# A two-layer diffusion backbone on one core: the first layer's context attention is interleaved with the first latent block, and some SBUF start addresses move by 128 bytes

## The chip, the cores and the metric

The kernel runs on one core of a Trainium2 chip, as one launch. The metric is device time in microseconds (us). The time before is the median of three runs, 3418.91 us (3416.81 to 3418.94).

The engines are TensorE (PE; its weight loads are listed as PEld), VectorE (DVE), ScalarE (ACT), GpSimd (POOL) and SyncE (SP, which here only issues DMAs). Each engine executes its own instructions in the order of the program.

## What is computed

The trunk has two layers over 1024 latent tokens, with 256 context tokens as a prefix; the model width is 1024, everything is float32. The change lies in layer 0. Its mixer projects the normalised tokens with one large weight, gives part of the columns to grouped-query attention (8 query heads of 64, 2 key heads) and part to a bidirectional gated scan (HGRN2), and multiplies both results with one output projection:

```python
def attend(q, k, v):
    s = jnp.einsum("bqhgd,bkhd->bhgqk", q, k).astype(jnp.float32) * ATTN_SCALE
    p = jax.nn.softmax(s, axis=-1).astype(v.dtype)
    return jnp.einsum("bhgqk,bkhd->bqhgd", p, v)
...
# latent queries: keys of context and latent; context queries: keys of the context alone
y_lat = jnp.concatenate([oa_lat, readout(ob_lat, bg_l)], axis=-1) @ w_out
y_ctx = jnp.concatenate([oa_ctx, readout(ob_ctx, bg_c)], axis=-1) @ w_out
```

So a context query sees 256 keys, and a latent query sees 1280.

## The kernel before

**Stages.** `even_in` normalises the tokens, projects them token by token (`even_token_major`) and then runs the HGRN2 scan (`hgrn`), which projects as it goes. `even_out` holds the attention and the output projection (`even_attention`). `middle` is the first ConvFFN and the entry of layer 1, `odd_out` its output projection, `last` the second ConvFFN. A float32 product is made of three fp32r matmuls (high by high, high by low, low by high), all recorded at the helper line L115.

**The attention (`even_attention`).** Queries come in five blocks of 256: block 0 is the context, blocks 1 to 4 the latents. A pair (b, h) is a block with a head; there are 40 pairs. Each pair takes two half-steps s, one for each 128 queries, and the loop over s from 0 to 87 is a software pipeline written out by hand (`in_order` keeps the order on every engine). In half-step s, in this order on each engine:

- `scores(s)` (L115, DVE L897): the score matmuls of half-step s into PSUM, then one DVE instruction that copies them into the tile `a_p` and gives the row's minimum `nm` (the queries were stored negated). A context half-step writes 256 columns into `g_ps`, of which there are two buffers; a latent one writes 1280 columns into `a_s`, of which there is one, so the next latent scores wait for this DVE instruction;
- `exponential(s-1)` (ACT L904);
- `prepare_w` (ACT L868, POOL L869) in some half-steps: one of eight pieces of the output weight is split into `w_hi` and `w_lo`;
- `values` (tile `a_pv`) for the pair three before;
- `transposes` (PE L930, ACT L931, DVE L932) for the pair two before: a latent half-step transposes ten 128 by 128 pieces in three groups through two PSUM buffers, a context pair four pieces in its first half-step and none in its second. Both halves of the pair must have been divided. Between the groups, `step` may pull work of the output projection;
- `divide(s-1)` (DVE L909, POOL L910): the reciprocal `rl` of the row sum, and one POOL instruction that multiplies all of `a_p` by it;
- `finish` (ACT L959, DVE L961) for the pair three before, in its second half-step, and entries of a list `todo`: `split` (ACT L950, POOL L951) for every second head, and four `gated` for the HGRN2 result once a block's last head is finished.

Six buffers of `a_p` let half-steps overlap.

**The projection as filler.** `project()` is a generator that yields after each three matmuls of the output projection; a block has 32 such yields. `step(n)` advances it, but never beyond the blocks whose `gated` entries have all run (`ready`). If a block's entries come due while the one before is still unfinished, `gated` first pulls the rest at once. The last block's 32 yields come after the loop.

**Order of the pairs before.** All eight context pairs come first (half-steps 0 to 15), then the latent blocks one after the other. The eight `prepare_w` lie in half-steps 2, 4, ... 16. The context block's last head (pair 7) is finished in half-step 21, its fourth `gated` runs in half-step 23, and the projection begins in half-step 24, with two yields in each half-step.

**Addresses.** In `mod_init` a tile `c_in` of 128 bytes per partition lies in the pool that comes ahead of `xh` and `xl`. In `even_attention` a tile `zeros` of 128 bytes (`LINE` is 32 floats) lies ahead of the keys, queries, probabilities and the other tiles of that stage.

Of the kernel before, what the change touches and what calls it, by code (L numbers as in the profile page):

```python
# [11 lines left out]
F32 = mybir.dt.float32  # L12
# [3 lines left out]
OP = mybir.AluOpType  # L16
# [4 lines left out]
P = 128  # L21
D = 1024
KT = D // P
# [7 lines left out]
AQ = 8  # L31
# [8 lines left out]
LINE = 32  # L40
# [21 lines left out]
class Trunk:  # L62
# [100 lines left out]
    def mod_init(self):  # L163
        nc, a = self.nc, self.a
        self.csil = self.mc.tile([P, KT, 32], F32, name="csil")
        c = self.mc.tile([P, KT, 4], F32, name="c_in")[:, :, 0:2]
        nc.sync.dma_start(c, a["cc"])
        nc.vector.memset(self.csil, 0.0)
        nc.scalar.activation(self.csil[:, :, 0:2], c, AF.Silu)
        self.bmt = self.mc.tile([P, DEPTH, 48], F32, name="bmt")  # L170
        nc.sync.dma_start(self.bmt, a["bmodT"])
        self.nrm = self.mc.tile([P, DEPTH, 2, KT], F32, name="nrm")
        nc.sync.dma_start(self.nrm, a["npreT"])
# [658 lines left out]
    def even_attention(self, gp, tp, pp, sp):  # L832
# [5 lines left out]
        nc, a = self.nc, self.a  # L838
        QB = 2 * P
        blocks = [(SEQ, 1)] + [(QB * i, 0) for i in range(4)]  # L840
        pairs = [(b, h) for b in range(len(blocks)) for h in range(AQ)]
        st = {}

        def load_q(i):
            if i < len(pairs):
                b, h = pairs[i]
                q2 = sp.tile([P, QB], F32R, name="a_q", bufs=3)
                nc.sync.dma_start(q2.bitcast(F32), self.q2d[h][:, blocks[b][0]:blocks[b][0] + QB].bitcast(F32))
                st["q", i] = q2

        def load_gate(kind):
            g = st["gate"] = sp.tile([P, D], F32, name="gate", bufs=1)
            nc.sync.dma_start(g, self.gated[0, 0, kind].partition_broadcast(P))
# [5 lines left out]
        def load_w(m):  # L859
            if m < 8:  # L860
                raws[m] = self.wp.tile([P, 1024], F32, name="w_raw", bufs=2)
                k = 2 * (m % 4)
                nc.sync.dma_start(raws[m].rearrange("p (a b) -> p a b", a=2), w_out[:, k:k + 2, 512 * (m // 4):512 * (m // 4) + 512])

        def prepare_w(m):
            raw = raws.pop(m)
            hi, lo = (self.wp.tile([P, 1024], F32R, name="w_" + x, bufs=8) for x in ("hi", "lo"))
            nc.scalar.copy(hi, raw)  # L868
            nc.gpsimd.tensor_tensor(out=lo, in0=raw, in1=hi.bitcast(F32), op=OP.subtract)  # L869
            W[m] = hi, lo  # L870
            load_w(m + 2)
# [3 lines left out]
        def load_keys(g):  # L875
            for s in range(2):
                k = K2[g, s] = sp.tile([P, NTOK], F32R, name=f"K2_{g}{s}", bufs=1)
                nc.sync.dma_start(k.bitcast(F32), self.k2d[g, s].bitcast(F32))
# [22 lines left out]
        def exponential(i):  # L901
            Pt, nm, nk = st["t", i]
            l = st["l", i] = self.small.tile([P, 1], F32, name="l")
            nc.scalar.activation(Pt[:, :nk], Pt[:, :nk], AF.Exp, bias=nm, scale=-1.0, accum_out=l)  # L904
# [43 lines left out]
        def split(b, k, oT):  # L948
            oh, ol = st["o", b, k] = [sp.tile([P, QB], F32R, name=f"a_o{x}", bufs=12) for x in "hl"]
            nc.scalar.copy(oh, oT)  # L950
            nc.gpsimd.tensor_tensor(out=ol, in0=oT, in1=oh.bitcast(F32), op=OP.subtract)  # L951

        def finish(pair):
            b, h = pairs[pair]
            pv = st["pv"]
            if h % 2 == 0:
                st["oT"] = sp.tile([P, QB], F32, name="a_oT", bufs=2)
            t = sp.tile([P, QB], F32, name="pv_t", bufs=1)[64:128]
            nc.scalar.copy(t, pv[64:128, :QB])  # L959
            r = 64 * (h % 2)  # L960
            nc.vector.tensor_tensor(out=st["oT"][r:r + 64], in0=pv[0:64, :QB], in1=t, op=OP.add)  # L961
            if h % 2 == 1:
                todo.append(lambda oT=st["oT"]: split(b, h // 2, oT))
            if h == AQ - 3:
                g = st["g", b] = self.wp.tile([P, BH, QB], F32, name="a_g", tag="w_raw", bufs=2)
                for k in range(BH):
                    nc.sync.dma_start(g[:, k, :], self.hgd[k][:, blocks[b][0]:blocks[b][0] + QB])
            if h == AQ - 1:
                todo.extend(lambda k=k: gated(b, k) for k in range(BH))

        def gated(b, k):

            step(32 * b - at[0])
            split(b, BH + k, st["g", b][:, k, :])
            if k == BH - 1:
                st["ready"] = b
# [37 lines left out]
        fill, todo, at = project(), [], [0]  # L1014

        def step(n):

            for _ in range(n):
                if at[0] < 32 * (st.get("ready", -1) + 1):
                    next(fill, None)  # L1020
                    at[0] += 1

        zeros = sp.tile([P, LINE], F32, name="zeros", bufs=1)[:, 0:1]
        nc.gpsimd.memset(zeros, 0.0)
        N = 2 * len(pairs)
        E = mybir.EngineType
        with self.in_order(*self.compute, E.SP):
            load_keys(0)
            load_q(0)
            load_q(1)  # L1030
            load_keys(1)
            V = sp.tile([P, NT, AKV * P], F32R, name="V2", bufs=1)
            nc.sync.dma_start(V.bitcast(F32), self.v2d.rearrange("t p c -> p t c").bitcast(F32))
            load_w(0)
            load_w(1)
            load_gate(1)
            for s in range(N + 8):
                pair, half = s // 2, s % 2
                if s < N:
                    if half == 0:  # L1040
                        load_q(pair + 2)
                    scores(s)
                if 0 <= s - 1 < N:
                    exponential(s - 1)
                if 2 <= s < 18 and half == 0:
                    prepare_w(s // 2 - 1)
                if 0 <= pair - 3 < len(pairs):
                    values(pair - 3, half)
                t = transposes(pair - 2, half) if 0 <= pair - 2 < len(pairs) else iter(())
                next(t, None)  # L1050
                step(1)
                next(t, None)
                step(1)
                next(t, None)
                if 0 <= s - 1 < N:
                    divide(s - 1)
                if 0 <= pair - 3 < len(pairs) and half == 1:
                    finish(pair - 3)
                for _ in range(min(len(todo), 1 + len(todo) // 3)):
                    todo.pop(0)()  # L1060
            while todo:
                todo.pop(0)()
            step(32)
            for _ in fill:
                pass
# [1257 lines left out]
```

## Time and profile before

| what | us |
| --- | --- |
| median of three runs | 3418.91 |
| the profiled execution's own time | 3424.98 |
| its span, first to last instruction | 3423.0 |
| span: PE busy | 3125.8 (91%) |
| stretch 692 to 728, context scores | PE 20.51, POOL 32.82 busy of 36.00 |
| stretch 728 to 757, first latent scores | PE 21.79, POOL 24.51 busy of 29.00 |
| stretch 757 to 1060, latent blocks with filler | PE 283.75, POOL 228.79 busy of 303.00 |

All times below are counted from the start of the span. A row of the timeline has the start, the duration, the engine, the line, the operation, the tile written and the tiles read, and in brackets the engine's idle time before it with what ended it. A row of groups ends in busy time, mean duration in ns, and idle time before. PEclk is the TensorE clock that was granted, as a share of full speed.

### The profile page before, as it was taken

The numbers are of one execution on the slowest core, as the hardware profiler recorded it, in microseconds if no ns is written. First come the engines' busy times: TensorE is split into PE (matmuls) and PEld (weight loads), VectorE is DVE, ScalarE is ACT, GpSimd is POOL, SyncE is SP. The second block draws the span as 40 slices with busy tenths as digits, with TensorE's granted clock in tenths as the row PEclk, the third lists the DMA queues.
The fourth block names the chain that finished last, engine by engine and source line by source line (L and its number), as shares of the span: only waits on it lengthen the run. The fifth ranks groups of instructions, "written<-read, shape, count | busy, mean of one in ns | idle before, by whom it ended". The sixth has DMA issues, their size and how long they took to land.

```text
span 3423.0 us, 48746 instructions
## 1 busy us (share of the span) xinstructions
PE 3125.8 (91%) x18364; PEld 2575.7 (75%) x18364; DVE 2057.6 (60%) x3413; ACT 1486.6 (43%) x2619; POOL 1524.0 (45%) x1147
## 2 busy tenths in 40 slices
PE   5999998869998699999999989999997679999997
PEld 3766776658887488888878768898986468888785
DVE  3625666647775754545577763476775565454778
ACT  3223222256664543434344442566664344443443
POOL 1310111187774466666610111677771167777201
PEclk8999999979999699999999989999998789999998
DMA  6533333221112221212285772222215412222756
GB/s 233 161 102 128 128 119 115 101 90 38 50 44 67 96 71 64 73 68 73 74 291 190 254 241 112 70 60 64 66 44 172 154 50 88 79 87 80 269 186 215
DMA packets 204844, 399.25 MB, mean 117 GB/s; under 512 B 24112, under 2 KB 86064, under 8 KB 204608
## 3 DMA queue, kind: packets, MB, share of 16 engines
q1 hardware_dynamic: 195552, 364.15, 32.6%
q0 software_dynamic: 9056, 31.99, 2.4%
q8 instruction: 144, 2.36, 0.3%
q14 instruction: 92, 0.75, 0.1%
HBM read 322.11 MB, written 74.34 MB: 116 GB/s over the span
## 4 chain that ended last, share of the span: by engine, by line
PE 74%; DVE 10%; DMA 4%; ACT 4%; issue 4%; POOL 2%; SPq 1%; POOLq 0%; ACTq 0%; DVEq 0%
PE g_ps L115 21%; PE u_g L115 13%; PE d_ps L115 10%; PE u_v L115 10%; PE u_pc L115 4%; PE c_pv L115 2%; PE a_pv L115 2%; PE c_s L115 2%; PE c_pt L2032 2%; PE a_pt L930 2%; PE mod_ps L115 1%; DVE a_pl L932 1%; PE a_s L115 1%; ACT a_ph L931 1%; DMA m_raw<-in_w_mod 1%
## 5 line engine op out<-in xcount | busy, mean ns | idle before, releaser
L123 POOL TENSOR_TENSOR rs_r<-rs_e,mhalf 128x1 f32<-128x1 f32 (+3 forms) x106 | 81.3, 767 | 1015.1 <-DVE rs_e L122 1014.8
L115 PE MATMUL d_ps<-d_Bh,d_Ah 128*128 128x512 f32 x704 | 277.3, 394 | 10.8 <-ACT d_Bh L1460 10.7
L115 PE MATMUL g_ps<-xh,w_hi 128*128 128x512 f32 (+1 forms) x704 | 277.0, 394 | 5.6 <-ACT w_hi L544 5.6
L115 PE MATMUL d_ps<-d_Bl,d_Ah 128*128 128x512 f32 x704 | 277.8, 395 | 3.9 <-DVE d_Bl L1461 3.4
L115 PE MATMUL d_ps<-d_Bh,d_Al 128*128 128x512 f32 x704 | 276.6, 393 | 2.0 <-DVE d_Al L1461 1.9
L910 POOL TENSOR_SCALAR a_p<-a_p,rl 128x1280 f32<-128x1280 f32 (+1 forms) x80 | 240.0, 3003 | 73.1 <-DVE rl L909 64.8
L2015 POOL TENSOR_SCALAR c_p<-c_p,rl 128x640 f32<-128x640 f32 (+1 forms) x128 | 230.8, 1805 | 86.0 <-DVE rl L2014 60.7
L115 PE MATMUL g_ps<-xh,w_lo 128*128 128x512 f32 (+1 forms) x704 | 257.2, 365 | 1.5 <-DVE w_lo L545 1.2
L115 PE MATMUL g_ps<-xl,w_hi 128*128 128x512 f32 (+1 forms) x704 | 256.9, 365 | 0.0
L1242 DVE TENSOR_TENSOR f_u<-u_v,f_p 128x512 f32<-128x512 f32 x88 | 60.5, 687 | 185.4 <-PE u_v L115 185.4
L932 DVE TENSOR_TENSOR a_pl<-a_pt,a_ph 128x512 fp32r<-128x512 f32 (+1 forms) x200 | 118.6, 602 | 85.7 <-ACT a_ph L931 85.3
L115 PEld LDWEIGHTS g_ps<-xh,w_hi 128*128 128x128 f32 x704 | 134.4, 191 | 44.7 <-issue 27.8
L115 PEld LDWEIGHTS d_ps<-d_Bh,d_Ah 128*128 128x128 f32 x704 | 133.6, 190 | 41.1 <-ACT d_Bh L1460 12.3
L115 PEld LDWEIGHTS d_ps<-d_Bl,d_Ah 128*128 128x128 f32 x704 | 133.5, 190 | 36.4 <-DVE d_Bl L1461 8.0
L1228 POOL TENSOR_TENSOR w_S4l<-w_s,w_S4h 128x512 fp32r<-128x512 f32 x44 | 57.0, 1295 | 230.4 <-ACT w_S4h L1227 230.4
L115 PE MATMUL g_ps<-w_hi,xh 128*128 128x512 f32 (+1 forms) x400 | 156.1, 390 | 2.2 <-DVE xh L1797 1.2
L115 PEld LDWEIGHTS d_ps<-d_Bh,d_Al 128*128 128x128 f32 x704 | 133.6, 190 | 30.8 <-DVE d_Al L1461 3.3
L931 ACT CAST a_ph<-a_pt 128x512 fp32r<-128x512 f32 (+1 forms) x200 | 102.8, 518 | 121.7 <-PE a_pt L930 121.4
L115 PE MATMUL g_ps<-w_lo,xh 128*128 128x512 f32 (+1 forms) x400 | 152.0, 380 | 2.7 <-DVE w_lo L1785 1.9
L115 PEld LDWEIGHTS g_ps<-xh,w_lo 128*128 128x128 f32 x704 | 133.7, 190 | 25.0 <-DVE w_lo L545 1.7
L115 PE MATMUL g_ps<-w_hi,xl 128*128 128x512 f32 (+1 forms) x400 | 152.1, 380 | 0.2 <-DVE xl L280 0.2
L2035 DVE TENSOR_TENSOR c_pl<-c_pt,c_ph 128x256 fp32r<-128x256 f32 (+1 forms) x256 | 113.0, 470 | 50.1 <-ACT c_ph L2034 48.9
(468 smaller groups left out, 9738.4 us busy)
## 6 DMA issues: line engine op xcount, KB each, us to landing
m_raw<-in_w_mod SPq DMA_DIRECT2D x96, 512.0 KB
w_raw<-in_w_up SPq DMA_DIRECT2D x88, 512.0 KB
d_rawA<-actd SPq DMA_DIRECT2D x77, 512.0 KB
d_rawB<-in_w_down SPq DMA_DIRECT2D x74, 512.0 KB
actd<-f_t SPq DMA_DIRECT2D x22, 640.0 KB
d_t<-in_w_down SPq DMA_DIRECT2D x22, 512.0 KB
actd<-f_t SPq DMA_DIRECT2D x22, 512.0 KB
d_s<-actd SPq DMA_DIRECT2D x20, 512.0 KB
```

The costliest lines, as they stand in the source:

```text
L115: return self.nc.tensor.matmul(out, lhsT, rhs, start=start, stop=stop, skip_group_check=True, **k)
L123: nc.gpsimd.tensor_tensor(out=r[:p, :n], in0=e[:p, :n], in1=self.mhalf[:p, :n], op=OP.pow)
L910: nc.gpsimd.tensor_scalar(Pt[:, :nk], Pt[:, :nk], rl, None, op0=OP.mult)
L930: nc.tensor.transpose(pt[:, m, qt * P:(qt + 1) * P], Pt[:, kts[j + m] * P:(kts[j + m] + 1) * P], self.ident)
L931: nc.scalar.copy(ph[:, j:j + n], pt[:, :n])
L932: nc.vector.tensor_tensor(out=pl[:, j:j + n], in0=pt[:, :n], in1=ph[:, j:j + n].bitcast(F32), op=OP.subtract)
L1228: nc.gpsimd.tensor_tensor(out=lo, in0=part(j, name), in1=hi.bitcast(F32), op=OP.subtract)
L1242: nc.vector.tensor_tensor(out=out, in0=x, in1=y, op=OP.add)
L2015: nc.gpsimd.tensor_scalar(Pt[:, :n], Pt[:, :n], rl, None, op0=OP.mult)
L2032: nc.tensor.transpose(pt[:, j, :], Pt[:, (src + j) * P:(src + j + 1) * P], self.ident)
L2035: nc.vector.tensor_tensor(out=vap(pl, o, dims), in0=pt[:, :cnt], in1=vap(ph, o, dims).bitcast(F32), op=OP.subtract)
```

## The change

```diff
-        c = self.mc.tile([P, KT, 4], F32, name="c_in")[:, :, 0:2]
+        c = self.wp.tile([P, 1024], F32, name="c_in", tag="w_raw", bufs=self.w_raw)[:, 0:2 * KT].rearrange("p (k s) -> p k s", s=2)
...
-        pairs = [(b, h) for b in range(len(blocks)) for h in range(AQ)]
+
+        pairs = [p for i in range(4) for p in ((0, 2 * i), (0, 2 * i + 1), (1, i))] + [(1, h) for h in range(4, AQ)]
+        pairs += [(b, h) for b in range(2, len(blocks)) for h in range(AQ)]
...
-                st["oT"] = sp.tile([P, QB], F32, name="a_oT", bufs=2)
+                st["oT", b] = sp.tile([P, QB], F32, name="a_oT", bufs=3)
...
-            nc.vector.tensor_tensor(out=st["oT"][r:r + 64], in0=pv[0:64, :QB], in1=t, op=OP.add)
+            nc.vector.tensor_tensor(out=st["oT", b][r:r + 64], in0=pv[0:64, :QB], in1=t, op=OP.add)
...
-                todo.append(lambda oT=st["oT"]: split(b, h // 2, oT))
+                todo.append(lambda oT=st["oT", b]: split(b, h // 2, oT))
...
-        zeros = sp.tile([P, LINE], F32, name="zeros", bufs=1)[:, 0:1]
+        zeros = sp.tile([P, 2 * LINE], F32, name="zeros", bufs=1)[:, 0:1]
...
-                if 2 <= s < 18 and half == 0:
-                    prepare_w(s // 2 - 1)
+                if 2 <= s < 26 and s % 3 == 2:
+                    prepare_w(s // 3)
...
-                step(1)
+                step(1 if at[0] >= 32 else 2)
```

The order of the first twelve pairs becomes: two context heads, one latent head of block 1, four times over; then block 1's other four heads, then blocks 2 to 4 as before. The eight `prepare_w` move to half-steps 2, 5, 8, ... 23. While the context's 32 yields last, a half-step takes three yields instead of two. A third buffer of `a_oT` lets the two blocks be under way together.

The numbering of half-steps stays, so their content changes: the twelve mixed pairs fill half-steps 0 to 23. The context's last head is pair 10 and is finished in half-step 27; its fourth `gated` runs in half-step 29, and the projection begins in half-step 30. In both programs pair 15 is the last of block 1, its first `gated` comes due in half-step 37, and from half-step 38 on the two programs are the same.

The start addresses of the tiles in SBUF, modulo 256 bytes, as the two programs have them:

| tiles | before | after |
| --- | --- | --- |
| weights `w_raw`, `w_hi`, `w_lo` and nearly all large tiles of the later stages | 128 | 128 |
| `xh`, `xl` of layer 0 | 0 | 128 |
| keys `K2`, `V2`, `a_q`, `a_p`, `a_ph`, `a_pl`, `a_oT`, `a_oh`, `a_ol`, `y`, `y_x` of the attention | 0 | 128 |
| HGRN2: `hA`, `hkt`, `hds`, `hS`, `h_dg`, `h_o` | 0 | 128 |
| HGRN2: `hF`, `hK`, `hQ`, `hT`, `hq`, `hKM`, `hV`, `hgate`, `ones` | 128 | 0 |

## The prediction

> **What bounds the kernel now.** I read the page first, then busy time by stretch, then POOL's groups, then the timeline where the context pairs give way to the latent ones. The page gives the span, PE's busy share and the chain that ended last.
>
> ```profile
> span 3423.0 us, 48746 instructions
> ...
> PE 3125.8 (91%) x18364; PEld 2575.7 (75%) x18364; DVE 2057.6 (60%) x3413; ACT 1486.6 (43%) x2619; POOL 1524.0 (45%) x1147
> ...
> PE 74%; DVE 10%; DMA 4%; ACT 4%; issue 4%; POOL 2%; SPq 1%; POOLq 0%; ACTq 0%; DVEq 0%
> ```
>
> PE bounds the whole, so what counts is where PE waits or runs slowly. The stretches, with the busy time of PE, PEld, DVE, ACT and POOL and then PEclk, show it:
>
> ```profile
> 200.00:245.00 45.00, 45.00 (x202) 35.53 (x201) 4.91 (x9) 6.49 (x12) 0.00 (x0) 1.00 0.21 71
> 300.00:420.00 120.00, 112.97 (x1297) 83.42 (x1295) 77.35 (x161) 35.93 (x66) 17.86 (x23) 1.00 0.38 122
> 692.00:728.00 36.00, 20.51 (x85) 16.79 (x84) 14.54 (x60) 21.40 (x53) 32.82 (x28) 0.63 0.54 179
> 728.00:757.00 29.00, 21.79 (x100) 17.96 (x100) 18.19 (x34) 17.25 (x32) 24.51 (x12) 0.76 0.11 33
> 757.00:1060.00 303.00, 283.75 (x1820) 245.76 (x1819) 224.97 (x410) 194.31 (x370) 228.79 (x100) 1.00 0.13 43
> ```
>
> The projections of layer 0 (first two rows) are PE-bound. The context's scores (692 to 728) are POOL-bound: 32.82 of 36.00, with PE busy 20.51 at a clock of 0.63. From 757 on, with the projection as filler, PE is busy 94% at full clock. The change touches the third and fourth rows by its order, and all five by its addresses.
>
> **The order.** After half-step 38 both programs are the same, so I compare when half-step 38 starts its scores. POOL's groups and the rows of the timeline that I use (in the first fence: shapes, count, busy us, mean ns):
>
> ```profile
> L910 POOL TENSOR_SCALAR a_p<-a_p,rl 128x1280 f32<-128x1280 f32 x64 | 225.4, 3522 | 71.7 <-DVE rl L909 63.4 <-ACT a_oh L950 8.1
> L869 POOL TENSOR_TENSOR w_lo<-w_raw,w_hi 128x1024 fp32r<-128x1024 f32 x8 | 18.9, 2365 | 0.3 <-ACT w_hi L868 0.3
> L951 POOL TENSOR_TENSOR a_ol<-a_oT,a_oh 128x256 fp32r<-128x256 f32 x20 | 14.7, 736 | 8.3 <-ACT a_oh L950 8.3
> L910 POOL TENSOR_SCALAR a_p<-a_p,rl 128x256 f32<-128x256 f32 x16 | 14.7, 929 | 1.4 <-DVE rl L909 1.4
> L868 ACT CAST w_hi<-w_raw 128x1024 fp32r<-128x1024 f32 x8 | 8.2, 1030 | 0.0
> ```
>
> ```profile
> 698.13 0.92 POOL L910 TENSOR_SCALAR a_p<-a_p,rl 128x256 f32<-128x256 f32 x1 [1.40 <-DVE rl L909]
> ...
> 702.12 0.77 PE L115 MATMUL g_ps<-K,a_q 128*128 128x256 f32 x2 [4.02 <-DMA a_q<-q2d]
> ...
> 745.79 2.48 PE L115 MATMUL a_s<-K,a_q 128*128 128x512 f32 x6
> ...
> 748.08 1.67 PE L930 MATMUL a_pt<-ident,a_p 128*128 128x128 f32 x8
> ...
> 750.78 1.40 PE L115 MATMUL a_s<-K,a_q 128*128 128x512 f32 x6
> ...
> 752.44 1.49 DVE L897 CUSTOM_DVE_ANT_0 a_p<-a_s,zeros 128x1280 f32<-128x1280 f32 x1
> ...
> 753.06 1.36 ACT L904 ACTIVATE a_p<-a_p,nm 128x1280 f32<-128x1280 f32 x1
> ...
> 753.75 1.04 PE L930 MATMUL a_pt<-ident,a_p 128*128 128x128 f32 x8
> ...
> 755.90 0.44 PE L930 MATMUL a_pt<-ident,a_p 128*128 128x128 f32 x2 [1.11 <-DVE a_pl L932]
> 756.09 1.40 PE L115 MATMUL a_s<-K,a_q 128*128 128x512 f32 x6
> ...
> 760.77 1.42 PE L115 MATMUL a_s<-K,a_q 128*128 128x512 f32 x6
> ...
> 764.10 0.48 PE L115 MATMUL g_ps<-w_hi,a_oh 128*128 128x512 f32 x1
> ...
> 835.97 1.32 PE L115 MATMUL a_s<-K,a_q 128*128 128x512 f32 x6
> ```
>
> Before: half-step 24 starts its scores at 760.77, its first filler runs at 764.10, and half-step 38 starts at 835.97. Without filler a latent half-step takes (760.77 - 750.78)/2 = 5.0. With two yields it takes little more: from 760.77 to 835.97 are 14 half-steps, less the four yields pulled at once in half-step 37 (next fence, 2.80, so 0.70 each), (75.20 - 2.80)/14 = 5.17.
>
> ```profile
> 833.34 2.80 PE g_ps L115 x12
> ```
>
> That is the flaw that I see in the new order: **a latent half-step without filler costs nearly as much as one with it.** It is held by a ring, not by PE's work: from the transpositions to the next scores are 756.09 - 753.75 = 2.34, with 1.11 of waiting for DVE; then 1.40 of scores and 1.49 of DVE. Before, the filler starts with 8 latent half-steps scored; after, with 14 (half-step 30), so six more run bare, and their yields are made up later.
>
> Step by step, after:
> 1. The first latent scores are half-step 4. Their query tile is the one that lands just before 702.12, so its DVE instruction ends about 702.1 + 1.4 + 1.5 = 705.0, and half-step 5 can start its scores, since `a_s` has one buffer.
> 2. From there: exp 1.36 with its row-sum read (about 0.2), `w_hi` 1.03, `w_lo` 2.37 on POOL ahead of the division, two divisions 2 x 3.52: 12.0, at 717.0. Only then can the pair be transposed (half-step 8). PE has two context pairs between, some 5 us of work, and waits for the rest.
> 3. Half-steps 8 and 9 transpose the latent pair beside context scores: about 2.9 each to the next scores (2.34 and 0.5 of context scores). Half-step 10's latent scores and their DVE instruction add 2.5 behind DVE's queue: 8.3, so half-step 11 starts at 725.3.
> 4. This repeats: half-step 17 at 725.3 + 12.8 + 8.3 = 746.4 (ACT has 0.8 of a context pair's copies ahead of the exp), half-step 23 another 21.1 later and 0.7 for the `a_ol` that then stands between the two divisions: 768.2. POOL's own work in such six half-steps is 4 x 0.93 + 2 x 3.52 + 2 x 2.37 + 0.74 = 16.2, so POOL would idle 5 of 21.
> 5. Pair 11 is transposed at 768.2 + 12.8 = 781.0, half-step 27 starts at 783.3, half-step 30 three bare ones later: 798.3.
> 6. Eight half-steps with three yields. The third adds at most its 0.70, and at least 0.70 less PE's idle share of a half-step, (303.00 - 283.75)/57 = 0.34: 5.5 to 5.9, I take 5.8: 46.4. Then 32 - 24 = 8 yields are pulled at once in half-step 37: 5.6. Half-step 38 starts at 850.3.
>
> So the order costs 850.3 - 836.0 = **14**. The bounds: if POOL never idled, its work from 698.13 up to the division of half-step 27 would be 16 x 0.93 + 12 x 3.52 + 8 x 2.37 + 6 x 0.74 = 80.5, half-step 30 could start at 776, and half-step 38 at 776 + 8 x 5.5 + 5.6 = 826: 10 gained. The other end is PE at half clock in those bursts (below): 21 lost. I take the ring's value, since the rows of the same ring (750.78 to 760.77) show it.
>
> The rest of the order costs nothing that I can find: SP is passed the same DMAs, and the output weight is ready by half-step 23, ahead of its first use in 30. The moved `w_lo` are the 2.37 of step 2: in their old places they were in the POOL-bound stretch too, and are counted once.
>
> **The addresses.** The chain of waits shows long runs of 512-column matmuls; the first of these runs has `xh` at 0 modulo 256, the second, in layer 1's entry, the same form with `xh` at 128 (the weights are at 128 in both):
>
> ```profile
> 233.36 16.82 PE g_ps L115 x72
> ```
>
> ```profile
> 2108.02 36.76 PE g_ps L115 x162
> ```
>
> These are 16.82/72 = 0.2336 and 36.76/162 = 0.2269 per matmul, both at full clock: 6.7 ns apart. Nothing else that I know differs in the two runs' instructions. The change puts `xh`, `xl`, the keys and `a_oh` to 128. Matmuls of 512 columns in layer 0's projections:
>
> ```profile
> L115 PE MATMUL g_ps<-xh,w_hi 128*128 128x512 f32 x256 | 109.4, 427 | 0.0
> ...
> L115 PE MATMUL g_ps<-w_hi,xh 128*128 128x512 f32 x160 | 64.8, 405 | 0.9 <-ACT w_hi L479 0.9
> ```
>
> With their two partners each that is 3 x 416 = 1248, times 6.7 ns = 8.4. The short runs inside HGRN2 get only part, so I take 7. The attention has another 736 (256 in the scores, 480 filler), 4.9 at most, but the ring holds there, and I count none. Bounds: 0, if the addresses aren't the reason, and 13. The HGRN2 tiles that go from 128 to 0 feed small matmuls only; no row tells their price, and I count nothing. The sum: 14 - 7 = **7 slower**.
>
> **Against the median.** The profiled execution took 3424.98, 1.98 more than its span; the median of the three runs is 3418.91, 6.07 lower. The sum is a difference inside one execution, so I add it to the median: 3426. About 0.2% (6.8 us) is what a measurement of this kernel can tell from no change.
>
> **Rivals.**
> - *Half clock in the mixed stretch (slower).* PEclk was 0.63 and 0.76 in the two stretches now mixed. At half clock scores take 2.48 instead of 1.40 and from transpositions to the next scores pass 750.78 - 748.08 = 2.70 instead of 2.34, so each group of six half-steps costs 1.1 + 2 x 0.4 = 2 more, and a few bare half-steps 1 each: 7 in all, 3433. For it: PE would be busy about half of each group, with a gap of some 5 us. Against it: the clock was full in 750 to 760 with such bare half-steps. The Trainium skill (TensorE: Matmul & The Clock Gate, "What's actually happening") says that an idle window of about 3.4 us throttles PE to half clock, and a busy one releases it; by that rule the gap of each group would throttle PE.
> - *POOL stays fed (not slower).* One mechanism: the division of the latent half-steps starts early enough that PE never waits for it, because POOL's queue is filled ahead by the six `a_p` buffers. It decides in step 2: if the transpositions of half-step 8 begin within 8 us of half-step 5's scores rather than 12, each group is 16 to 17 instead of 21, half-step 38 comes at 829 to 832, 4 to 7 early; with the addresses 3406. For it: POOL ran without a gap from 698 to 733 before. Against it: `rl` of each division stands behind the transpositions' DVE work.
> - *The addresses do nothing (slower).* The 6.7 ns come from something else in layer 0, and the order's 14 stand alone: 3433. The Trainium skill (same page, "Wait — 56ns, not 53.3ns?") gives the warm spacing of matmuls as columns over 2.4 GHz plus 2.5 ns, by my estimate 216 ns for 512, and knows no address; the two runs above, 234 and 227, agree neither with that nor with each other.
>
> **How the numbers follow.** My forecast as worked out, 3426: 0.40, its own spread half below and half above 0.2%. Half clock 0.18, slower. Addresses without effect 0.12, slower. POOL fed 0.30, nearly all faster (0.27). So faster 0.27, within 0.2% 0.23, slower 0.50. The range, 3405 to 3437, reaches from the fed POOL to the half clock with weak addresses.
>
> **What would show it.** Right: in the new profile the latent transpositions of half-steps 8, 14, 20 wait for POOL `a_p` L910, the mixed groups take about 21 us each, half-step 30's first filler runs near 800, half-step 38's scores start about 14 later than 835.97 less what was gained ahead, and a run of 72 matmuls near 233 takes 16.3. Wrong: groups of 17 or less, or filler before 790 would mean the ring was misread; a run of 72 still at 16.8 would mean that the addresses are not the cause; PEclk of 0.5 through the groups is the first rival.

## The result and the profile after

The changed kernel is slower: its median of five runs is 3437.70 us against 3418.91, and the ratio is 1.0052 (95% interval 1.0040 to 1.0065, that is 14 to 22 us). One of the five runs was disturbed (6420.15); the other four took 3431.36 to 3438.56, with their middle at 3435.6. The profiled execution took 3431.36, with a span of 3429.5. The page's span and busy times, after:

```profile
span 3429.5 us, 48743 instructions
...
PE 3111.9 (91%) x18364; PEld 2566.0 (75%) x18364; DVE 2060.2 (60%) x3413; ACT 1487.1 (43%) x2619; POOL 1524.7 (44%) x1147
```

PE is busy 13.9 us less than before (3125.8), and yet the span is longer, so PE waits more. The stretches shown of before, after the change (PE, PEld, DVE, ACT, POOL, then PEclk), and two more within the last one:

```profile
200.00:245.00 45.00, 45.00 (x207) 36.31 (x206) 4.08 (x8) 6.38 (x11) 0.00 (x0) 1.00 0.23 77
300.00:420.00 120.00, 113.98 (x1337) 84.09 (x1336) 80.42 (x165) 36.36 (x66) 19.22 (x25) 1.00 0.40 127
692.00:728.00 36.00, 22.42 (x102) 18.77 (x103) 17.18 (x49) 19.53 (x40) 23.77 (x17) 0.67 0.35 115
728.00:757.00 29.00, 15.54 (x92) 12.80 (x90) 13.12 (x37) 16.34 (x36) 23.09 (x13) 0.85 0.25 78
757.00:1060.00 303.00, 275.16 (x1733) 237.68 (x1734) 217.72 (x398) 188.40 (x361) 227.47 (x103) 0.99 0.14 46
```

```profile
765.00:798.00 33.00, 23.56 (x149) 19.77 (x149) 22.74 (x44) 21.85 (x42) 28.07 (x14) 1.00 0.07 21
798.00:850.00 52.00, 50.83 (x306) 43.82 (x305) 33.73 (x62) 30.22 (x58) 37.02 (x18) 1.00 0.17 52
```

The first row shows the addresses: in the same 45 us PE got through 207 recorded matmuls instead of 202. The fourth shows the order: PE is busy 15.54 of 29.00, where it had been 21.79, and POOL isn't full either (23.09). From 765 to 798 PE is still idle for 9.4 of 33 us; from then on, with the filler, it is busy 50.83 of 52.00.

What PE waited for between 692 and 765, by the view of waits (total, times, longest):

```profile
PE a_pt L932 <- POOL a_p L912: 11.2, 5, 3.9
PE a_pv L115 <- DVE a_oT L963: 9.6, 6, 2.5
PE a_s L115 <- DMA a_q<-q2d: 4.0, 1, 4.0
```

The timeline of PE after shows where: a latent pair's transpositions (tile `a_pt`) wait for POOL's division once in each group of six half-steps.

```profile
697.91 2.50 PE L115 MATMUL a_s<-K,a_q 128*128 128x512 f32 x6 [4.01 <-DMA a_q<-q2d]
702.00 2.50 PE L115 MATMUL a_s<-K,a_q 128*128 128x512 f32 x6 [0.74 <-DVE nm L899]
713.87 1.75 PE L932 MATMUL a_pt<-ident,a_p 128*128 128x128 f32 x7 [3.16 <-POOL a_p L912]
...
723.45 1.43 PE L115 MATMUL a_s<-K,a_q 128*128 128x512 f32 x6
...
736.12 1.75 PE L932 MATMUL a_pt<-ident,a_p 128*128 128x128 f32 x7 [3.17 <-POOL a_p L912]
...
745.37 1.41 PE L115 MATMUL a_s<-K,a_q 128*128 128x512 f32 x6
...
758.78 1.76 PE L932 MATMUL a_pt<-ident,a_p 128*128 128x128 f32 x7 [3.86 <-POOL a_p L912]
...
768.27 1.41 PE L115 MATMUL a_s<-K,a_q 128*128 128x512 f32 x6
...
781.01 0.98 PE L932 MATMUL a_pt<-ident,a_p 128*128 128x128 f32 x7 [1.29 <-POOL a_p L912]
783.21 1.41 PE L115 MATMUL a_s<-K,a_q 128*128 128x512 f32 x6
...
797.13 1.41 PE L115 MATMUL a_s<-K,a_q 128*128 128x512 f32 x6
800.47 0.48 PE L115 MATMUL g_ps<-w_hi,a_oh 128*128 128x512 f32 x1
...
849.18 1.30 PE L115 MATMUL a_s<-K,a_q 128*128 128x512 f32 x6
```

The `a_s` rows at 702.00, 723.45, 745.37 and 768.27 are half-steps 5, 11, 17 and 23; those at 783.21, 797.13 and 849.18 are 27, 30 and 38. The groups take 21.9 and 22.9 us. POOL's own rows for the first of them show what PE waits for. `w_lo` stands ahead of the pair's two divisions, which end at 706.79 + 2 x 3.52 = 713.83, and PE goes on at 713.87 (the third of the row's x3 is a context division behind them):

```profile
704.45 2.38 POOL L871 TENSOR_TENSOR w_lo<-w_raw,w_hi 128x1024 fp32r<-128x1024 f32 x1 [0.68 <-ACT w_hi L870]
706.79 7.92 POOL L912 TENSOR_SCALAR a_p<-a_p,rl 128x1280 f32<-128x1280 f32 x3
```

To compare the attention alone I use the first instruction of VectorE's minimum as a mark (the first one, half-step 0, and the one of half-step 38). Timeline of before, then of after:

```profile
696.76 0.42 DVE L897 CUSTOM_DVE_ANT_0 a_p<-g_ps,zeros 128x256 f32<-128x256 f32 x1 [2.37 <-POOL zeros L1024]
...
837.44 1.49 DVE L897 CUSTOM_DVE_ANT_0 a_p<-a_s,zeros 128x1280 f32<-128x1280 f32 x1 [2.72 <-PE a_s L115]
```

```profile
692.44 0.42 DVE L899 CUSTOM_DVE_ANT_0 a_p<-g_ps,zeros 128x256 f32<-128x256 f32 x1 [2.37 <-POOL zeros L1026]
...
850.52 1.49 DVE L899 CUSTOM_DVE_ANT_0 a_p<-a_s,zeros 128x1280 f32<-128x1280 f32 x1 [3.19 <-PE a_s L115]
```

So 4.3 us are gained ahead of the attention, and from half-step 0 to half-step 38 it takes 158.1 instead of 140.7: 17.4 lost. From half-step 38 to the last one, 79, both take 217 us. What follows half-step 79 is the same work in all kernels; it took 2368.5 in the profiled execution of before and 2359.0 to 2365.5 in the thirteen others. The 6 us by which before's profiled execution stood above its median may well lie there; in any case it is why the two profiled spans are only 6.5 apart, while the attention ends 13.1 later.

### The profile page after: what moved, and what is told of

Its sections match the earlier page's. It is cut to its first block, busy times and chain, and to the rows that moved or that the text cites. A ratio compares the mean times of both kernels' runs of the same rounds, so it can differ in the third digit from the quotient of the medians.

```text
span 3429.5 us, 48743 instructions
## 1 busy us (share of the span) xinstructions
PE 3111.9 (91%) x18364; PEld 2566.0 (75%) x18364; DVE 2060.2 (60%) x3413; ACT 1487.1 (43%) x2619; POOL 1524.7 (44%) x1147
## 3 DMA queue, kind: packets, MB, share of 16 engines
q8 instruction: 144, 2.36, 0.3%
## 4 chain that ended last, share of the span: by engine, by line
PE 72%; DVE 10%; issue 5%; DMA 4%; ACT 4%; POOL 3%; SPq 0%; POOLq 0%; ACTq 0%; DVEq 0%
PE g_ps L115 19%; PE u_g L115 13%; PE d_ps L115 10%; PE u_v L115 10%; PE u_pc L115 4%; PE a_pv L115 2%; PE c_pv L115 2%; PE c_s L115 2%; PE a_pt L932 2%; PE c_pt L2034 2%; PE mod_ps L115 1%; DVE a_pl L934 1%; PE a_s L115 1%; ACT a_ph L933 1%; DMA y_x<-x2d 1%
```

## The experiments

Each kernel was profiled once and timed against the kernel before on the same chip. The marks of the minimum give, in us of the trace: the first one, then the time from half-step 0 to 24 (the mixed or the context's stretch), 24 to 30, 30 to 38, and 0 to 38.

| kernel | first | 0-24 | 24-30 | 30-38 | 0-38 | ratio to before |
| --- | --- | --- | --- | --- | --- | --- |
| before | 696.8 | 65.7 | 30.6 | 44.4 | 140.7 | 1 |
| after | 692.4 | 80.6 | 25.8 | 51.7 | 158.1 | 1.0052 |
| e1_order | 700.5 | 80.5 | 27.0 | 51.8 | 159.3 | 1.0060 |
| e2_addr | 696.6 | 63.8 | 30.6 | 44.3 | 138.7 | 0.9991 |
| e3_wlo | 695.2 | 76.0 | 25.6 | 51.7 | 153.4 | 1.0034 |
| e4_late | 699.7 | 63.6 | 29.8 | 51.8 | 145.2 | 1.0027 |
| e5_div_act | 694.9 | 78.2 | 25.6 | 51.7 | 155.6 | 1.0043 |
| e9_both | 698.4 | 85.7 | 25.3 | 51.7 | 162.7 | 1.0072 |
| e6_half_line | 698.1 | 64.0 | 30.7 | 44.5 | 139.2 | 0.9998 |
| e7_lo_dve | 695.5 | 63.3 | 30.6 | 44.3 | 138.2 | 0.9985 |
| e10_short_div | 696.9 | 64.3 | 24.2 | 51.7 | 140.3 | 0.9999 |
| e11_pv2 | 695.5 | 64.3 | 30.6 | 44.3 | 139.2 | 0.9989 |
| e12_pv2_lo | 694.0 | 65.2 | 30.6 | 44.3 | 140.2 | 0.9989 |
| e13_twos | 691.9 | 68.7 | 30.3 | 48.0 | 147.0 | 1.0011 |

**The two halves of the change, apart.** e1_order is the changed kernel with the old `c_in` and `zeros`:

```diff
-        c = self.wp.tile([P, 1024], F32, name="c_in", tag="w_raw", bufs=self.w_raw)[:, 0:2 * KT].rearrange("p (k s) -> p k s", s=2)
+        c = self.mc.tile([P, KT, 4], F32, name="c_in")[:, :, 0:2]
...
-        zeros = sp.tile([P, 2 * LINE], F32, name="zeros", bufs=1)[:, 0:1]
+        zeros = sp.tile([P, LINE], F32, name="zeros", bufs=1)[:, 0:1]
```

> The changed kernel with the old addresses (c_in and zeros as before), so the new order alone. Theory (the ring makes the mixed half-steps and the bare ones long; the addresses help apart from it): half-step 38 starts its scores 14 to 18 later, counted from the first scores, than in the kernel before; the time is 14 to 20 above before, and a run of 72 matmuls near 233 us still takes 16.8. Rival (the order is neutral and the slowness comes from the new addresses): within 3 of before.

Measured: 3436.07 (3435.55 to 3444.62) against 3418.61, ratio 1.0060 (1.0048 to 1.0073): 17.5 above. In the trace half-step 38 comes 159.3 after the first scores, 18.6 later than before and a little past the 14 to 18 expected. e2_addr is the kernel before with only those two lines new.

> The kernel before with the new addresses alone (c_in and zeros). Theory: 4 to 5 gained by the time the attention starts, as in the trace of the changed kernel, little in the attention, so 3 to 7 below before; a run of 72 matmuls takes 16.4. Rival (the addresses cost something later, as the timed runs of the changed kernel lie further above before than its profile does): 0 to 6 above before.

Measured: 3413.49 (3406.72 to 3421.34), ratio 0.9991 (0.9981 to 1.0000): 5.1 by the medians, 3 by the ratio, with an interval that reaches 1.0000. One expected sign is missing: the first scores come only 0.2 earlier than before in this trace, and not 4 to 5. The order is the whole loss, and the addresses gain a little at most.

**When the filler starts.** e4_late keeps the order and the addresses of before, but holds the projection until half-step 30, with three yields from there, as after the change:

```diff
-                if at[0] < 32 * (st.get("ready", -1) + 1):
+                if at[0] < 32 * (st.get("ready", -1) + 1) and st["s"] >= 30:
...
+                st["s"] = s
...
-                step(1)
+                step(1 if at[0] >= 32 else 2)
```

> The kernel before in its old order and addresses, but the filler waits until half-step 30 and then runs at three yields a half-step, as in the changed kernel; no context pair is moved. Theory (bare half-steps cost as much as filled ones): half-step 38 starts 6 to 9 later than in the kernel before, and the time is 6 to 9 above before. Rival (the third yield hides in PE's idle time): within 2 of before, and the whole cost is the mixed stretch.

Measured: 3426.58 (3425.07 to 3435.14), ratio 1.0027 (1.0015 to 1.0040): 8 above, as expected. In the trace half-steps 30 to 38 take 51.8, the same as after the change (51.7), instead of 44.4; up to half-step 30 nothing is lost. Half-step 38 comes only 4.5 later than before, less than the 6 to 9 expected, chiefly because half-steps 0 to 24, which this kernel leaves as they were, took 63.6 here and 65.7 in before's trace. Why the same filler costs more there is seen in e2_addr's stretch from 765 to 798, which holds filler, beside the two rows of after shown above:

```profile
765.00:798.00 33.00, 32.17 (x211) 28.31 (x211) 23.64 (x44) 21.17 (x40) 24.49 (x9) 1.00 0.12 35
```

PE is busy 32.17 of 33.00 there, and 23.56 in the same stretch after the change: 8.6 us of PE's time that the early filler used and the late one leaves empty, to be made up at 50.83 of 52.00.

**POOL's queue.** e3_wlo moves the eight `prepare_w` of the changed kernel from half-steps 2, 5, 8, ... to those in which no latent division is due:

```diff
-                if 2 <= s < 26 and s % 3 == 2:
-                    prepare_w(s // 3)
+                if 2 <= s < 22 and s % 6 in (2, 3):
+                    prepare_w(2 * (s // 6) + s % 6 - 2)
```

> The changed kernel, but the eight pieces of the output weight are split in half-steps 2, 3, 8, 9, 14, 15, 20, 21, so that no w_lo stands on POOL ahead of a latent pair's two divisions. Theory (POOL's queue between the exp and the transpositions is the ring): each of the four waits shortens by up to 2.4, 7 to 9 below the changed kernel. Rival (POOL isn't what holds the mixed groups, but PE at half clock): within 2 of the changed kernel.

Measured: 3430.10 (3427.29 to 3430.45), ratio 1.0034 (1.0022 to 1.0047): 7.6 below the changed kernel, as expected, but only 4.7 nearer in the trace. PE's wait for POOL falls from 11.2 to 6.8. `w_lo` ahead of the divisions is part of the wait. The next two take POOL out by other means. e5_div_act, on the changed kernel:

```diff
-            nc.gpsimd.tensor_scalar(Pt[:, :nk], Pt[:, :nk], rl, None, op0=OP.mult)
+            if i < 24 and nk == NTOK:
+                nc.scalar.activation(Pt[:, :nk], Pt[:, :nk], AF.Copy, scale=rl)
+            else:
+                nc.gpsimd.tensor_scalar(Pt[:, :nk], Pt[:, :nk], rl, None, op0=OP.mult)
```

> The changed kernel, with the eight divisions of the first latent block's first four pairs (POOL a_p by rl, 128x1280, 3.52 us each) made by ScalarE instead; the exponential of the same size takes ScalarE 1.37 us. POOL ring theory (the mixed groups last as long as the way from a latent half-step's scores over POOL to the pair's transpositions): the way of each of four groups becomes shorter by 2 x (3.52 - 1.5) = 4 us and more where w_lo stands ahead of it, so 10 to 16 below the changed kernel's 3437.7 in the median, that is 3422 to 3428, and the four waits of a_pt for POOL's a_p are gone. Rival (half clock, the a_q transfers or PE's own order set the groups): within 3 of the changed kernel.

Measured: 3434.20 (3431.24 to 3440.43), ratio 1.0043 (1.0029 to 1.0057): hardly better than the changed kernel, 2.5 nearer in the trace. The expected time was missed. The waits of e5_div_act's PE from 690 to 775 say why:

```profile
PE a_pv L115 <- DVE a_oT L966: 21.3, 8, 6.0
PE a_pt L935 <- DVE a_pl L937: 4.0, 6, 0.8
```

The wait of `a_pt` for POOL is gone, as expected, but `a_pv` now waits 21.3 for `a_oT`, where it had waited 9.9 in the same stretch of the changed kernel. There is one `a_pv`, and it comes free when ScalarE has copied it and VectorE has added it. ScalarE does its work in order, and the copy (`pv_t`) now stands behind divisions that wait for their `rl`. The timeline of e5_div_act shows it for the longest of these waits: values that PE wrote from 705.83 on are copied at 713.34.

```profile
705.83 0.28 PE L115 MATMUL a_pv<-a_ph,V 128*128 128x256 f32 x1
...
707.40 1.36 ACT L913 ACTIVATE a_p<-a_p,rl 128x1280 f32<-128x1280 f32 x1 [0.70 <-DVE rl L911]
...
711.47 1.36 ACT L913 ACTIVATE a_p<-a_p,rl 128x1280 f32<-128x1280 f32 x1 [0.89 <-DVE rl L911]
...
713.34 0.37 ACT L964 COPY pv_t<-a_pv 64x256 f32<-64x256 f32 x1
...
713.74 0.42 DVE L966 TENSOR_TENSOR a_oT<-a_pv,pv_t 64x256 f32<-64x256 f32 x1 [0.23 <-ACT pv_t L964]
...
714.30 0.55 PE L115 MATMUL a_pv<-a_ph,V 128*128 128x256 f32 x1 [6.05 <-DVE a_oT L966]
```

One wait took the place of the other.

e9_both is e5_div_act with `w_lo` on VectorE as well:

```diff
-            nc.gpsimd.tensor_tensor(out=lo, in0=raw, in1=hi.bitcast(F32), op=OP.subtract)
+            nc.vector.tensor_tensor(out=lo, in0=raw, in1=hi.bitcast(F32), op=OP.subtract)
```

> As the run with ScalarE's divisions, and in addition the eight subtractions of w_lo (2.36 us each on POOL) on VectorE. POOL ring theory: another 2 to 6 below that run, so 3417 to 3426, since POOL then has only the 256-wide divisions in these groups. If the mixed order brings anything of its own once POOL is out of the way, it shows here as a time below that of the old order with the new addresses (3413.5). Rival (the order costs by PE's queue order itself): no more than 3 below the run with the divisions alone, and above 3420.

Measured: 3445.48 (3439.97 to 3449.02), ratio 1.0072 (1.0058 to 1.0087), worse than the changed kernel, and a miss in the same direction: half-steps 0 to 24 take 85.7. Its chain of waits has VectorE's `w_lo` between ScalarE's `w_hi` and the division:

```profile
755.90 0.95 ACT w_hi L870
756.87 1.23 DVE w_lo L871
758.26 1.36 ACT a_p L913
```

That this is why it is slower still is argued from the chain; no run shows it apart.

These two runs could not tell whether POOL's time or the way through all the queues sets the groups, since they moved work. e10_short_div takes work away and moves nothing:

```diff
+            if i < 24:
+                nk = CTX
             nc.gpsimd.tensor_scalar(Pt[:, :nk], Pt[:, :nk], rl, None, op0=OP.mult)
```

> The changed kernel, with the division of the first twelve pairs' rows cut to their first 256 columns: the eight POOL divisions of 128x1280 become 128x256, 0.93 us instead of 3.52, and nothing is moved to another engine (the other 1024 columns of these rows stay undivided, so part of the computation is left out). Theory after the run with ScalarE's divisions: the mixed groups are bound by the whole way of a latent pair through the engines' queues (scores, minimum, exponential, division, transposition, cast, values, a_oT), in which POOL is the longest link, so 8 x 2.6 = 20.7 us taken from that link show for the most part: half-step 38's scores 10 to 18 nearer to the first ones than in the changed kernel (158.1), and the median 10 to 18 below 3437.7. Rival (the way over ScalarE and VectorE, with the one a_pv buffer, is as long by itself): half-step 38 at 153 to 157, median within 5 of 3437.7.

Measured: 3419.30 (3411.99 to 3424.88), ratio 0.9999 (0.9988 to 1.0010). 20.7 us less on POOL brought half-step 38 nearer by 17.8 and the median down by 18.4, both at about the upper end of what was expected. The stretch from 728 to 757 of e10_short_div beside after's row:

```profile
728.00:757.00 29.00, 19.13 (x131) 15.90 (x130) 18.94 (x50) 20.63 (x47) 19.74 (x18) 1.00 0.32 101
```

No engine is full there either. The clock is full throughout (0.85 in after's row), so the 17.8 hold both the waits and the half clock that went with them. The length of POOL's division does set the groups; that it does so as a link in a chain, and not by its sum, the next run shows.

**What the latent pair has for cover.** e13_twos is the changed kernel with the same twelve pairs in two groups of four context and two latent pairs:

```diff
-        pairs = [p for i in range(4) for p in ((0, 2 * i), (0, 2 * i + 1), (1, i))] + [(1, h) for h in range(4, AQ)]
+        pairs = [p for i in (0, 2) for p in [(0, 2 * i + j) for j in range(4)] + [(1, i), (1, i + 1)]] + [(1, h) for h in range(4, AQ)]
```

> The changed kernel with its twelve mixed pairs in two groups of four context pairs and two latent pairs, instead of four groups of two and one; nothing else differs, POOL's work is the same in sum (some 65 us in these 24 half-steps). If what costs is that only two short half-steps stand between a latent pair's scores and its transpositions, so that PE waits out POOL's two divisions: the first latent pair of each group now has the second one's two half-steps as cover, two of the four exposed waits go, and half-step 38's scores come 148 to 153 us after the first ones (158.1 in the changed kernel); median 3427 to 3432. Rival (POOL's work in sum sets the stretch, wherever the pairs stand): 156 to 160, median within 4 of 3437.7.

Measured: 3423.51 (3414.79 to 3427.72) against 3418.72, ratio 1.0011 (0.9999 to 1.0023); half-step 38 comes 147.0 after the first scores. Both are a little better than the theory expected, and far from its rival. The wait for POOL from 690 to 765 shrinks from 11.2 to this row of e13_twos:

```profile
PE a_pt L932 <- POOL a_p L912: 0.4, 1, 0.4
```

POOL's work is the same in sum; where the pairs stand decides. What is left against e2_addr in the trace is 8.3; 3.7 of it lie in half-steps 30 to 38 (48.0 against 44.3), where this kernel's filler, too, has to catch up.

**The addresses.** e6_half_line has the order of before, and puts the tiles that had stood at 0 modulo 256 to 64 or 192 instead of 128:

```diff
-        c = self.mc.tile([P, KT, 4], F32, name="c_in")[:, :, 0:2]
+        c = self.mc.tile([P, KT, 2], F32, name="c_in")
...
-        zeros = sp.tile([P, LINE], F32, name="zeros", bufs=1)[:, 0:1]
+        zeros = sp.tile([P, 3 * LINE // 2], F32, name="zeros", bufs=1)[:, 0:1]
```

> The order of before; c_in stays in its pool with 64 bytes and zeros has 192, so that the operands which stood at 0 modulo 256 stand at 64 or 192 (1984 matmuls of 512 columns), and the others at 128 as ever. If only the place 0 modulo 256 is slow: spacing 227 ns in all, the run of 72 near 233 us takes 16.4, and the time is 3 to 7 below before. If 128 modulo 256 is the only fast place: spacing 232 to 234 where one operand stands at 64 or 192, the run of 72 takes 16.8, and the time is that of before within 2.

Measured: 3420.00 (3410.47 to 3424.20) against 3420.26, ratio 0.9998 (0.9989 to 1.0008). The run of 72 that the prediction quoted (16.82 before), and the one ahead of it (16.93 before), in the chain after the change, then in that of e6_half_line:

```profile
214.72 16.56 PE g_ps L115 x72
...
231.72 16.37 PE g_ps L115 x72
```

```profile
218.05 16.99 PE g_ps L115 x72
...
235.48 16.82 PE g_ps L115 x72
```

With `xh` at 128 the second run takes 227.4 ns per matmul. At 192 it takes 233.6, and its 16.82 are to the hundredth what it took at 0; e1_order, with the old places, has 16.82 as well, and e2_addr 16.36. In these runs `xh` is the stationary operand, the one that is loaded as weights (128*128 in a row), and of the places tried for it (0, 192, 128) only 128 is fast. Where `xh` is the moving operand (128x512), 192 turned out as good as 128: the expected 232 to 234 did not come, but 230.1 (last section).

**In search of a version that beats both.** Two things stand out in the context's stretch of e2_addr, in its busy times and in its waits:

```profile
696.00:732.00 36.00, 22.75 (x92) 19.49 (x92) 16.16 (x63) 24.52 (x57) 34.09 (x27) 0.57 0.58 185
```

```profile
PE a_pv L115 <- DVE a_oT L961: 6.5, 4, 1.6
```

POOL is busy 34.09 of 36.00, and PE waits for the one value buffer. The next three kernels go at these two. e7_lo_dve takes e2_addr and puts `w_lo` on VectorE (the line of e9_both).

> The order of before with the new addresses (3413.5 by itself), and the eight subtractions of w_lo on VectorE instead of POOL. In the stretch of the context's pairs POOL is busy 34.1 of 36 us, and a pair takes 4.5 us, of which POOL's two divisions and one w_lo are 1.83 + 2.36. If POOL bounds the context's stretch: a pair becomes 3.1 to 3.9 us, eight of them 5 to 10 us shorter, so 3404 to 3409. Rival (the transfers of w_raw, 512 KB a pair, or the chain from scores to values bound it just as closely): within 2 of 3413.5.

Measured: 3413.79 (3409.30 to 3421.55) against 3420.26, ratio 0.9985 (0.9976 to 0.9994). It is faster than before, but the addresses alone did that: half-step 38 comes at 138.2, and in e2_addr at 138.7. That is the rival's outcome: 2.36 us a pair less on POOL gained 0.5 in all, so POOL alone does not bound the context's stretch. e11_pv2 takes e2_addr and lets values alternate between two buffers:

```diff
-                st["pv"] = pp.tile([P, 512], F32, name="a_pv", bufs=1)
+                if blocks[b][1] and h in (0, 2, 4):
+                    st["pv"] = pp.tile([P, NT * P], F32, name="a_s", bufs=1)[:, :512]
+                else:
+                    st["pv"] = pp.tile([P, 512], F32, name="a_pv", bufs=1)
```

> The order of before with the new addresses (3413.5 by itself), and the context pairs of heads 0, 2 and 4 collect their values in the idle a_s banks, so that two value buffers alternate there. In that stretch PE waits each pair 1.6 us for a_oT, which frees the one a_pv buffer. If that ring bounds a context pair's 4.3 to 4.5 us: half-step 14 comes 3 to 6 us earlier after the first scores than in that run (27.0), and the median is 3408 to 3411. If POOL is just as close (34.1 of 36 us busy): within 2 of 3413.5 and half-step 14 within 1 of 27.0.

Measured: 3416.84 (3411.97 to 3420.44) against 3418.37, ratio 0.9989 (0.9979 to 0.9998). Half-step 14 comes 26.6 after the first scores, not 3 to 6 us earlier than e2_addr's 27.1. The wait for `a_oT` is gone, and the view of waits of e11_pv2 has another in its place:

```profile
PE g_ps L115 <- DMA a_q<-q2d: 4.2, 1, 4.2
PE a_pt L930 <- POOL a_p L910: 3.3, 5, 1.2
```

The first row stands in e2_addr's view too; the second was 0.4 there. e12_pv2_lo does both.

> Both: two value buffers in the context's stretch, and w_lo on VectorE instead of POOL, with the old order and the new addresses. If POOL's chain and the value buffer bound the stretch side by side, so that relieving one alone brings nothing: half-step 14 comes 5 to 9 us nearer to the first scores than 27.0, and the median is 3404 to 3409. Rival (ScalarE's and VectorE's queues, with PE at half clock, bound it too): half-step 14 at 25 to 27, median 3411 to 3415.

Measured: 3415.28 (3411.85 to 3420.80), ratio 0.9989 (0.9979 to 0.9999). Half-step 14 is at 25.6 instead of e2_addr's 27.1, but half-step 38 at 140.2 instead of 138.7. The 1.5 us gained with the context's pairs are given back by the first latent ones, which is about the rival's outcome. None of the three gains over e2_addr; the fastest that was found is the old order with the new addresses. Its gain is small, but the three that share it bear it out: their ratios are 0.9985 and twice 0.9989, with intervals that end below 1.

## Why the prediction was right in its sign and short in its size

**The ring of the mixed groups (steps 1 to 5): right, and mis-sized by about 4 us.** The transpositions of half-steps 8, 14 and 20 wait for POOL as the prediction said, and e10_short_div and e13_twos show that it is this wait: taken away in the one by shorter divisions, in the other by cover. Step by step, with the 4.3 us gained ahead added to the measured times, so that both count from the same first scores:

| half-step's scores | predicted | measured + 4.3 | off by |
| --- | --- | --- | --- |
| 5 | 705.0 | 706.3 | 1.3 |
| 11 | 725.3 | 727.8 | 2.5 |
| 17 | 746.4 | 749.7 | 3.3 |
| 23 | 768.2 | 772.6 | 4.4 |
| 27 | 783.3 | 787.5 | 4.2 |
| 30 | 798.3 | 801.4 | 3.1 |
| 38 | 850.3 | 853.5 | 3.2 |

So the order cost 17.4 by the marks instead of 14. Most of the 1.3 at the start is a term that was too small: the wait of 4.0 us for the query's DMA was in the sum, but the first latent scores then ran at half clock (2.50 instead of 1.4). The other 3 come at about 1 us a group. They fit the rival of half clock, which was partly true: the clock was half in each burst after a wait for POOL, and full between. After, by stretches:

```profile
720.80:734.50 13.70, 8.20 (x54) 6.89 (x53) 7.46 (x21) 8.90 (x18) 10.37 (x6) 1.00 0.19 57
734.50:741.30 6.80, 4.58 (x19) 3.73 (x19) 2.41 (x7) 2.63 (x6) 5.70 (x4) 0.50 0.10 14
741.30:754.90 13.60, 8.75 (x57) 7.44 (x57) 8.70 (x23) 10.23 (x21) 8.79 (x6) 1.00 0.28 100
754.90:765.20 10.30, 5.29 (x23) 4.43 (x23) 3.49 (x8) 3.22 (x7) 7.97 (x5) 0.50 0.19 57
```

The rival had priced a group at 2 us more and the latent half-steps behind at 1 each; the clock was full in those, and a group cost about half of that. That the half clock is what makes up these 3 us is argued from the rows; no run changed the clock alone. The Trainium skill (TensorE: Matmul & The Clock Gate, "What's actually happening") says that an idle window of some 3.4 us brings the half clock and a busy one of the same length ends it. The waits for POOL were of about that length, 3.16, 3.17 and 3.86, but the trace does not show them as what brought the half clock. The granted clock fell at 710.6, 734.5 and 754.9, and the waits began at 710.7, 733.0 and 754.9; ahead of each, PE had already waited 2.4, 2.0 and 2.5 for `a_oT`. The clock came back at 720.8, 741.3 and 765.2, which is 6.9, 5.2 and 6.4 after the waits ended. That is longer than one window of 3.4, but PE had two short idle times of about 0.6 in each of these stretches.

**Bare latent half-steps (step 5's 5.0 and the flaw named in the prediction): only partly right.** That filler which starts six half-steps later has to be paid for is right, and e4_late shows it apart. But the six half-steps from 24 to 30 took 25.8, 4.3 each, not 5.0, probably because they begin with the pipeline nearly drained: half-steps 24 to 26 start their scores 3.1 us apart. That is why the table's difference shrinks from 4.4 to 3.1 between half-steps 23 and 30. In the old order e4_late's bare half-steps 24 to 30 took 29.8 / 6 = 5.0 each, as the prediction had it.

**Three yields and eight at once (step 6): right.** 46.4 and 5.6 were forecast, 52.0 in all; from 797.13 to 849.18 are 52.05.

**The addresses: the cause right, the size too high.** The run of 72 went from 16.82 to 16.37 (16.3 was forecast), and nothing was gained within the attention: from half-step 38 to 79 it is 217 in both. But 7 was forecast, and 4.3 came in this pair of traces. Over all ten kernels with the new places the first mark is at 695.1 on average (691.9 to 698.4), over the four others at 698.8 (696.8 to 700.5): 3.7. The failing term is 6.7 ns for each of 1248 matmuls. It came from one run of 72 in which `xh` is the stationary operand. The 480 (3 x 160) matmuls of that kind went from 232.8 ns to 227.6 by the traces of before and after, but the other 768 (3 x 256), in which `xh` moves, only from 232.3 to 229.9 (last section). An estimate from these means is 480 x 5.2 + 768 x 2.4 ns = 4.3 us, about what came.

**POOL stays fed; the addresses do nothing.** Both rivals fell: PE did wait for POOL in every group, while e10_short_div shows what never waiting would have been worth, some 18 us; and the runs of 72 in e1_order, e2_addr and e6_half_line follow the addresses and nothing else. One reading of the prediction fell too, that the context's scores are POOL-bound: e7_lo_dve took 8 x 2.36 us off POOL in that stretch and gained 0.5.

**Against the median.** 17.4 less 4.3 is 13.1 at the end of the attention, and 3418.91 + 13.1 would be 3432. Forecast were 3426 and a range up to 3437. Measured are a median of 3437.7 and, by the ratio, 1.0052 x 3418.91 = 3436.7. So the time stands at the very end of the range. That end was made of half clock and weak addresses, and both came in part. The two errors of size, the order's 14 and the addresses' 7, went the same way, and that they did not carry the time clearly past the range is partly luck.

Of the 5 us or so between 3432 and these times, about 2 lie in the profiled execution of before, whose half-steps 0 to 24 took 65.7. In e2_addr, e4_late and e6_half_line, which leave these half-steps as they were, they took 63.6 to 64.0. PEclk from 737 to 751 was 0.63 in before and 0.88 in e2_addr and e4_late, so the first latent half-steps of before ran longer at half clock. Against e2_addr, which has the same addresses, the order costs 158.1 - 138.7 = 19.4. The rest stays open: the four runs spread over 7 us, and e1_order's profiled execution was itself 5.7 above its median.

## What to carry to other kernels

When short and long pieces of work are mixed in a software pipeline whose depth is counted in steps, the cover of a long piece shrinks with its neighbours: here a latent pair had two short steps between its scores and its transpositions, and PE paid for the 7 us of division on another engine that a row of long pairs had hidden. Move such a link to another in-order engine only after looking at what stands behind it in that queue: the wait went from POOL's division to the one value buffer. And filler is worth what PE idles where it stands: the same 32 yields were nearly free from half-step 24 and cost 7 us from half-step 30.

## What the runs showed of the hardware

The pace of 512-column fp32r matmuls can depend on the start address of their operands. The table has the mean spacing, in ns, of neighbouring records at full clock (spacings up to 260 ns), for the same matmuls in three traces. Ahead of each mean stands the place modulo 256 bytes of the operand named; the other operand is a weight at 128 in the first three rows.

| operand (records before) | before | e6_half_line | after |
| --- | --- | --- | --- |
| `xh`, `xl` stationary, layer 0's projections (444) | 0: 232.8 | 192: 233.3 | 128: 227.6 |
| `a_oh`, `a_ol` stationary, filler (259) | 0: 230.9 | 64: 232.3 | 128: 227.7 |
| `xh`, `xl` moving, layer 0's projections (596) | 0: 232.3 | 192: 230.1 | 128: 229.9 |
| `a_q` stationary and `K` moving, latent scores (126) | 0: 231.7 | 64: 231.4 | 128: 232.3 |

For the stationary operand of the projections 128 is fast and 0, 64 and 192 are not. The moving operand loses 2.4 at 0, and 192 is as good as 128. The scores show no dependence at all. Nor does the place explain every slow stretch: in layer 1, from 2144 to 2531, matmuls of the form `g_ps<-xh,w_hi` took 233.2 before and 233.3 after, though `xh` stands at 128 there in both programs (the prediction names it). All records of 512 columns outside the table have a mean of 227.5 in both traces (6880 and 6884 records). The attention's value matmuls of 256 columns (119 ns) and its transpositions (109 ns) took the same before and after, though their operands had moved from 0 to 128. Why 128 is the fast place no run shows.

The granted clock changed on a coarse grid: after the change, from 693.5 to 765.2, the stretches between two changes were 13.7, 3.4, 10.2, 13.7, 6.8, 13.7 and 10.2 us, all near multiples of 3.4.
